# Group norm statistics with tokens on partitions, a first norm that multiplies by its weights in rows, and a new order of the mixer's pieces

## The chip, the cores and the metric

The kernel runs on one core of a Trainium2 chip. The metric is device time in microseconds (us) of one execution. TensorE (PE, with PEld for its weight loads), VectorE (DVE), ScalarE (ACT), GpSimd (POOL) and SyncE (SP, which here only issues DMAs) each work through a queue of their own; data moves between HBM and on-chip memory by DMA.

## The reference

One encoder layer on x of 512 tokens by 1024 channels, all float32. Cut to what matters here:

```python
def rmsnorm(x, w):
    y = x * rsqrt(mean(x * x, axis=-1) + 1e-5)
    return y * w

h = rmsnorm(x, norm1_w)
p = h @ w_in                      # 1024 -> 2464: r, k, v, decay, a, gate, pool
# token shift of the RWKV columns, RWKV-7 scan in two directions (8 heads of 64),
# multi-scale pooling of the last 512 columns
y = wkv(...)                      # (tokens, 8 heads, 64)
y = (y - y.mean(-1)) / sqrt(y.var(-1) + 64e-5) * ln_x_w + ln_x_b   # per token and head
y = (y + bonus) * g               # g: a gate from two small products
x = x + concat(y, pooled) @ w_out
# then RMSNorm, a PEER layer (16384 single-neuron experts, top 16 of 8 heads),
# residual, final RMSNorm
```

## The kernel before

The mixer (up to about 435 us of the span) holds activations with channels on partitions and the 512 tokens along the free axis, in four token tiles x0 to x3 of 128. Matrices that must be exact are split into a high part and the rest, and a product is the sum of three passes: `wh*hh`, `wh*hl`, `wl*hh`.

**Norm 1 (lines 224 to 245).** Per token tile: ACT squares the 128x1024 tile and sums it (L234), `rstd_of` makes 1/rms out of it (L153 on DVE, L155 a square root on ACT, L157 on DVE), DVE multiplies the tile by it (L236), PE turns it over in eight 128x128 transposes, DVE multiplies by norm1_w out of PSUM into `hf` (L242), ACT rounds `hf` to `hh` (L244) and DVE or POOL, by a string, makes `hl = hf - hh` (L245). This block has no order of its own: the framework's scheduler places it. The last tile's L236 comes behind much of the other tiles' work.

**The mixer's streams.** After norm 1 the mixer is a set of generators, each of which issues one piece of work per step. A string PROG names, letter by letter, which generator takes its next step, and within it PE, DVE, ACT, SP and POOL keep exactly that order. The letters that matter here:

- `m`: the 20 column tiles of the input projection ("products", L338 to L342, in the order PORD; weight fetch L325, split L332 on ACT and L335 on DVE or POOL by the string WL). `0` to `3`: elementwise work of one of four head pairs (ct), in two directions (string EW says which of its operations go to POOL). `p`: pooling.
- `s`/`S`: the triangular solves of head pairs 0 and 1 / 2 and 3. They load AU from DRAM (L599) and do 31 pairs of small DVE steps (L607, L609). `j`/`J`: what is joined to them on PE.
- `h`: four gates (L857, L858, copied by ACT in L859). `l`: w_out (wo) and the residual (xr) by DMA on POOL's queue. `f`, `o`, `X`, `Y`: the output projection (L843) by parts.
- `a`, `b`: the two chains of eight chunks (L731 to L795; each chunk needs GA and UV from DRAM), of heads 0 to 3 and 4 to 7. `n`, `x`, `y`: group norm of heads 0 to 3 for all 512 tokens (`n`), of heads 4 to 7 for the middle 256 tokens (`x`) and for the outer 256 (`y`).

**Group norm (L806 to L835).** Mean by a matmul with `bm`, subtracted (L815); squares on ACT (L820); the sums over each head's 64 channels by a matmul with `hsel` as stationary operand (L821), which leaves heads on partitions: 8 x 512 or 8 x 256. On it DVE adds eps (L824), ACT takes the root (L825), DVE the reciprocal (L826). A matmul with `hselT` (L830) spreads it over the channels, times ln_x_w; L832 to L834 apply it, with ln_x_b, bonus and gate.

The PEER part behind the mixer is about 1275 us of the span and isn't touched.

Of the kernel before, what the change touches and what calls it, by code (L numbers as in the profile page):

```python
# [10 lines left out]
F32 = mybir.dt.float32  # L11
# [4 lines left out]
AF = mybir.ActivationFunctionType  # L16
# [42 lines left out]
WL = 'VVVGVGGGGVGVVVGVGVGG'  # L59
EW = 'VVGVVVVVVGVVGVGVVGVGVVVGVGGVVVGVGVGVGGGGVVVGGGVGGGVG'  # L60
# [100 lines left out]
def mixer(ctx, rs, tc, t, x_dram, x2_dram, ident, vec, vecs, dbg, load_vectors):  # L161
# [56 lines left out]

    with ExitStack() as s1:
        ld = s1.enter_context(tc.tile_pool(name="ld", bufs=1, side="right"))  # L220
        st = s1.enter_context(tc.tile_pool(name="st", bufs=NST, side="right"))
        x = [ld.tile([128, D], F32, name=f"x{i}") for i in range(NT)]
        XQ = {"S": (SY, SY), "A": (SY, A)}[QX]

        one = st.tile([128, 1], F32, name="one", bufs=1)
        V.memset(one, 1.0)
        A.activation(one, one, AF.Sqrt)
        for i in range(NT):
            XQ[i % 2].dma_start(x[i], x_dram[:, i])
        load_vectors()  # L230
        for i in range(NT):
            sc = st.tile([128, D], F32, name="sc", bufs=2)
            ssq = st.tile([128, 1], F32, name="ssq")
            A.activation(sc, x[i], AF.Square, accum_out=ssq)  # L234
            r = rstd_of(nc, st, ssq, "n1", 1.0 / D, RMS_EPS, 1)
            (G if SX[i] == "G" else V).tensor_scalar(x[i], x[i], r, None, op0=ALU.mult)  # L236
            for q in range(2):
                pt = bank([128, 4, 128])
                for d in range(4):
                    PE.transpose(pt[:, d], x[i][:, (4 * q + d) * 128:(4 * q + d + 1) * 128], ident)  # L240
                hf = st.tile([128, 4, 128], F32, name="hf", bufs=NHF)
                V.tensor_tensor(hf, pt, vecs("n1")[:, 4 * q:4 * q + 4, None].to_broadcast([128, 4, 128]), op=ALU.mult)  # L242
                part = lambda z: z[:, 4 * q:4 * q + 4, i * 128:(i + 1) * 128]
# [13 lines left out]
    rkh = mc.tile([128, 4], F32, name="rkh")
    V.tensor_scalar(rkh, vecs("rk"), 0.5, None, op0=ALU.mult)
    mln2 = mc.tile([128, 1], F32, name="mln2")
    V.memset(mln2, -float(np.log(2.0)))  # L260

    cmask = mc.tile([128, NC, C], F32, name="cmask")
    V.memset(cmask, 1.0)
    V.memset(cmask[:, :, 0:1], 0.0)
    cmaskf = cmask.rearrange("p c t -> p (c t)")

    gm = mc.tile([128, 2, C], F32, name="gm")
    V.memset(gm, 1.0)
    for hf in range(2):
        for k in range(2):  # L270
            G.affine_select(gm[hf * 64:hf * 64 + 64, k, :], gm[hf * 64:hf * 64 + 64, k, :], [[1, C]], ALU.is_ge, 0.0,
                            base=-1 if k == 0 else 0, channel_multiplier=-1)
    gmask = gm.rearrange("p k t -> p (k t)")


    hsel = mc.tile([128, 4, H], F32, name="hsel")
    sel2 = mc.tile([128, 2], F32, name="sel2")
    seli = mc.tile([128, 4, 8], F32, name="seli")
    bones = mc.tile([128, 128], F32, name="bones")
    for z in (hsel, sel2, seli, bones):  # L280
        G.memset(z, 0.0)
    for hf in range(2):
        rows = slice(hf * 64, hf * 64 + 64)
        V.memset(sel2[rows, hf:hf + 1], 1.0)
        V.memset(bones[rows, hf * 64:hf * 64 + 64], 1.0)
# [1323 lines left out]
```

## Time and profile before

| | |
|---|---|
| runs | 1709.47, 1710.9, 1721.64 us; median 1710.9 |
| profiled execution | 1711.15 us, span 1709.4 us, mean granted clock 0.962 |
| busy over the span | PE 1586.8 us (93%), DVE 1288.1 (75%), ACT 668.9 (39%), POOL 520.4 (30%) |
| first projection's first matmul | 21.90 us |
| solve 0 | steps from 187.56 us |
| chain 0, chain 1 | from about 291 us, from about 356 us |
| last output projection ends | about 435 us |

A row of the timeline gives the start, the duration, the engine, the line and the operation with its output and input; brackets give the engine's idle time before it and what ended that. Where matmuls stand one behind another a row's time is that of the whole run. The granted clock (PEclk) is a share of TensorE's 2.4 GHz; the two levels are 1.2 and 2.4 GHz, and a value between is a stretch with both.

### The profile page before, as it was taken

The numbers are of one execution on the slowest core, as the hardware profiler recorded it, in microseconds if no ns is written. First come the engines' busy times: TensorE is split into PE (matmuls) and PEld (weight loads), VectorE is DVE, ScalarE is ACT, GpSimd is POOL, SyncE is SP. The second block draws the span as 40 slices with busy tenths as digits, with TensorE's granted clock in tenths as the row PEclk, the third lists the DMA queues.
The fourth block names the chain that finished last, engine by engine and source line by source line (L and its number), as shares of the span: only waits on it lengthen the run. The fifth ranks groups of instructions, "written<-read, shape, count | busy, mean of one in ns | idle before, by whom it ended". The sixth has DMA issues, their size and how long they took to land.

```text
span 1709.4 us, 26365 instructions
## 1 busy us (share of the span) xinstructions
PE 1586.8 (93%) x9809; PEld 1326.2 (78%) x9809; DVE 1288.1 (75%) x2595; ACT 668.9 (39%) x1115; POOL 520.4 (30%) x359
## 2 busy tenths in 40 slices
PE   6898557989999699999999999999999999999997
PEld 5676444564787478988898989999998989999886
DVE  5557777346689999996567777877778877887776
ACT  4455322121333377774333333333333333333334
POOL 2313242000122000011024544445445555454430
PEclk8899778998999899999999999999999999999999
DMA  3344469671321365567979988989988998886774
GB/s 133 110 144 117 131 168 313 166 240 54 116 84 58 107 246 212 207 234 273 327 246 330 341 302 331 338 296 333 345 309 322 345 327 304 318 327 239 274 259 154
DMA packets 220193, 405.32 MB, mean 237 GB/s; under 512 B 38352, under 2 KB 137168, under 8 KB 216992
## 3 DMA queue, kind: packets, MB, share of 16 engines
q1 hardware_dynamic: 179536, 257.53, 45.7%
q0 software_dynamic: 39952, 145.05, 23.2%
q8 instruction: 77, 1.26, 0.3%
q10 hardware_dynamic: 576, 1.05, 0.2%
q14 instruction: 52, 0.43, 0.1%
HBM read 350.23 MB, written 53.35 MB: 236 GB/s over the span
## 4 chain that ended last, share of the span: by engine, by line
PE 63%; DVE 19%; DMA 5%; issue 1%; ACT 1%; SPq 1%; POOL 0%; DVEq 0%; ACTq 0%
PE o L1456 30%; PE d L1029 7%; PE d L1028 7%; PE d L1027 7%; PE mm L843 3%; DMA gt<-gdram 2%; DVE ul L1015 2%; DVE a L1256 1%; DMA UV<-vd 1%; DVE b L1258 1%; DVE bh L1260 1%; DVE pr L1530 1%; DVE tmf L607 1%; DVE i L1489 1%; DVE i L1486 1%
## 5 line engine op out<-in xcount | busy, mean ns | idle before, releaser
L1027 PE MATMUL d<-hh,uh 128*128 128x384 f32 x968 | 329.3, 340 | 0.3 <-ACT uh L1013 0.3
L1029 PE MATMUL d<-hh,ul 128*128 128x384 f32 x968 | 328.2, 339 | 1.1 <-DVE ul L1015 1.1
L1028 PE MATMUL d<-hl,uh 128*128 128x384 f32 x968 | 327.0, 338 | 0.0
L1373 POOL DMA_INDIRECT gat<-in_peer_u,num x128 | 192.3, 1502 | 291.7 <-DVE gat L1379 238.6
L1373 POOL DMA_INDIRECT gat<-in_peer_v,num x128 | 199.2, 1556 | 212.8 <-DVE acc L1381 193.2
L1456 PE MATMUL o<-vh,wh 128*128 128x512 f32 x768 | 238.4, 392 | 2.3 <-ACT wh L1440 2.3
L1456 PE MATMUL o<-vl,wh 128*128 128x512 f32 x768 | 238.5, 392 | 1.6 <-DVE vl L1015 1.5
L1456 PE MATMUL o<-vh,wl 128*128 128x512 f32 x768 | 238.6, 392 | 0.0
L1013 ACT CAST uh<-ur 128x1024 fp32r<-128x1024 f32 x121 | 127.2, 1051 | 258.9 <-PE d L1028 254.1
L1440 ACT CAST wh<-gl 128x384 fp32r<-128x384 f32 x128 | 65.7, 514 | 308.4 <-PE o L1456 297.3
L1028 PEld LDWEIGHTS d<-hl,uh 128*128 128x128 f32 x968 | 182.1, 188 | 4.2
L1027 PEld LDWEIGHTS d<-hh,uh 128*128 128x128 f32 x968 | 182.1, 188 | 3.9 <-ACT uh L1013 0.5
L1029 PEld LDWEIGHTS d<-hh,ul 128*128 128x128 f32 x968 | 182.1, 188 | 2.1 <-DVE ul L1015 1.8
L1442 DVE TENSOR_TENSOR wl<-gl,wh 128x384 fp32r<-128x384 f32 x128 | 71.3, 558 | 139.5 <-ACT wh L1440 139.4
L1015 DVE TENSOR_TENSOR ul<-ur,uh 128x1024 fp32r<-128x1024 f32 x121 | 147.7, 1221 | 37.1 <-ACT uh L1013 36.5
L1456 PEld LDWEIGHTS o<-vl,wh 128*128 128x128 f32 x768 | 144.1, 188 | 34.5 <-DVE vl L1015 3.1
L1456 PEld LDWEIGHTS o<-vh,wl 128*128 128x128 f32 x768 | 144.5, 188 | 31.2
L1381 DVE SCALAR_TENSOR_TENSOR acc<-gat,wg,acc 128x1024 f32<-128x1024 f32 x128 | 163.9, 1280 | 0.9
L1456 PEld LDWEIGHTS o<-vh,wh 128*128 128x128 f32 x768 | 143.6, 188 | 26.6 <-ACT wh L1440 2.6
L1015 DVE TENSOR_TENSOR vl<-vr,vh 128x1024 fp32r<-128x1024 f32 x128 | 156.2, 1221 | 8.5 <-ACT vh L1013 8.1
L1379 DVE SCALAR_TENSOR_TENSOR gat<-gat,h2g 128x1024 f32<-128x1024 f32 x128 | 153.6, 1219 | 0.0
L1013 ACT CAST vh<-vr 128x1024 fp32r<-128x1024 f32 x128 | 135.1, 1055 | 23.2 <-DMA vr<-in_peer_v 21.3
(374 smaller groups left out, 2457.8 us busy)
## 6 DMA issues: line engine op xcount, KB each, us to landing
ur<-in_uT SPq DMA_DIRECT2D x128, 512.0 KB, 5.0
vr<-in_peer_v SPq DMA_DIRECT2D x128, 512.0 KB, 3.6
gdram<-sg SPq DMA_DIRECT2D x24, 1024.0 KB, 5.6
gt<-gdram SPq DMA_DIRECT2D x16, 1536.0 KB, 11.3
wqk<-in_wqk SPq DMA_DIRECT2D x16, 576.0 KB, 3.8
gad<-gs SPq DMA_DIRECT2D x16, 512.0 KB, 3.5
GA<-gad SPq DMA_DIRECT2D x16, 512.0 KB, 5.7
w<-in_w_in SPq DMA_DIRECT2D x15, 512.0 KB, 4.8
```

The costliest lines, as they stand in the source:

```text
L843: PE.matmul(ps, (ocm if d < 4 else ypool)[:, d % 4, i * 128:(i + 1) * 128], wo[:, d, h], start=d == ds[0], stop=d == ds[-1])
L1013: A.copy(hi, src)
L1015: eng.tensor_tensor(lo, src, hi, op=ALU.subtract)
L1027: PE.matmul(ps, uh[:, c], hh[:, d, 0:ND], start=d == 0, stop=False)
L1028: PE.matmul(ps, uh[:, c], hl[:, d, 0:ND], start=False, stop=False)
L1029: PE.matmul(ps, ul[:, c], hh[:, d, 0:ND], start=False, stop=d == DT - 1)
L1373: G.indirect_dma_start(out=u, out_offset=None, in_=t["peer_u" if k < NP else "peer_v"], in_offset=bass.IndirectOffsetOnAxis(ap=num[:, kk:k ...
L1379: V.scalar_tensor_tensor(u, u, 1.0, h2g, op0=ALU.mult, op1=ALU.mult, accum_out=dot[:, kk:kk + 1])
L1381: V.scalar_tensor_tensor(acc, u, wg[:, kk:kk + 1], acc, op0=ALU.mult, op1=ALU.add)
L1440: A.copy(wh, w)
L1442: wi = V.tensor_tensor(wl, w, wh, op=ALU.subtract)
L1456: PE.matmul(O[j][q], a[:, c], b[:, q * 512:(q + 1) * 512], start=e == 0 and n == 0, stop=e == NE - 1 and n == 2)
```

## The change

What it does:

1. **Norm 1.** norm1_w is loaded as a row repeated over 128 partitions (`n1`, 512 KB, the second DMA on SP, ahead of x1). One DVE instruction per tile multiplies by 1/rms and by `n1`. `hf` is gone: ACT copies `hh` straight out of PSUM, DVE makes `hl` out of PSUM and `hh`; none goes to POOL. The block gets an order: all four `normed`, then tiles 0 and 1 turned over, the first weight split, tiles 2 and 3. The first weight fetches come ahead of the small constants.
2. **The first product** is done in two halves of 256 columns (48 matmuls of 128x256 for 24 of 128x512), and by passes, so that the first half needs tiles 0 and 1 alone.
3. **Group norm.** The squares are the stationary operand and `sel2` (128x2) the moving one: tokens on partitions, 128x8 for 256 tokens of four heads. Then eps, root, reciprocal on 128x8, a transpose to 8x128, an ACT copy, and four matmuls with `gselT`. A piece is always 256 tokens, so `n` has two pieces.
4. **A new PROG**, with other WL, EW, PORD and BP. Group norm's pieces stand further ahead among the chunks of chain 1.

```diff
-WL = 'VVVGVGGGGVGVVVGVGVGG'
+WL = 'VVVGVVGGGGGVVVGVGVGG'
-PORD = [12, 13, 4, 0, 8, 15, 5, 1, 2, 6, 16, ...
+PORD = [12, 13, 4, 0, 8, 15, 5, 1, 6, 2, 16, ...
-BP = 'GAGAVAVV'
+BP = 'GAGGVAVG'
-PROG = '...mwmmvpggvDjpjjSSSSSSSSSChhSSSSSlaSSSSlffffff...
+PROG = '...mwmpmvgvDpjjChhhjSSSSSSSSSSSSSSSSSSSlShhalffffff...
...
-            r = rstd_of(nc, st, ssq, "n1", 1.0 / D, RMS_EPS, 1)
-            (G if SX[i] == "G" else V).tensor_scalar(x[i], x[i], r, None, op0=ALU.mult)
-            for q in range(2):
...
-                hf = st.tile([128, 4, 128], F32, name="hf", bufs=NHF)
-                V.tensor_tensor(hf, pt, vecs("n1")[:, 4 * q:4 * q + 4, None].to_broadcast([128, 4, 128]), op=ALU.mult)
-                A.copy(part(hh), hf)
-                (G if SH[2 * i + q] == "G" else V).tensor_tensor(part(hl), hf, part(hh), op=ALU.subtract)
+        n1 = st.tile([128, D], F32, name="n1w", bufs=1)
+        SY.dma_start(x[0], x_dram[:, 0])
+        SY.dma_start(n1, bass.AP(tensor=t["norm1_w"].tensor, offset=t["norm1_w"].offset, ap=[[0, 128], [1, D]]))
+        for i in range(1, NT):
+            SY.dma_start(x[i], x_dram[:, i])
+        fetch(PORD[0])
+        load_vectors()
+        fetch(PORD[1])
+        with in_order(tc, V.engine, A.engine, PE.engine):
+            def normed(i):
...
+                V.scalar_tensor_tensor(x[i], x[i], r, n1, op0=ALU.mult, op1=ALU.mult)
+            def turned_over(i):
+                for q in range(2):
...
+                    A.copy(part(hh), pt)
+                    V.tensor_tensor(part(hl), pt, part(hh), op=ALU.subtract)
+            turned(selT, seli)
+            for i in range(NT):
+                normed(i)
+            for i in range(NT):
+                if i == 2:
+                    ready[PORD[0]] = weights(PORD[0])
+                turned_over(i)
...
+    def early_product(wh, wl, ps):
+        for n in range(2):
+            c = slice(n * 256, n * 256 + 256)
+            for k, (w, h) in enumerate(((wh, hh), (wl, hh), (wh, hl))):
+                for d in range(DT):
+                    PE.matmul(ps[:, c], w[:, d], h[:, d, c], start=k == d == 0, stop=k == 2 and d == DT - 1)
...
-            sq = wo_p.tile([128, 512], F32, name="sq2", bufs=2)
+            sq = wo_p.tile([128, 256], F32, name="sq2", bufs=2)
             A.activation(wide(sq), part(ocm[:, ct]), AF.Square)
-            PE.matmul(pv_[0:H, :n], hsel[:, ct, :], sq[:, :n], start=ct == cts[0], stop=ct == cts[1])
+            for k in range(2):
+                PE.matmul(pv_[:, k, ct % 2], sq[:, k * 128:(k + 1) * 128], sel2, start=True, stop=True)
-        nr = wo_p.tile([H, 512], F32, name="nr2")[:, :n]
-        V.tensor_scalar(nr, pv_[0:H, :n], 1.0 / N, GN_EPS, op0=ALU.mult, op1=ALU.add)
+        nr = wo_p.tile([128, 8], F32, name="nr2")
+        V.tensor_scalar(nr, pv_.rearrange("p i c h -> p (i c h)"), 1.0 / N, GN_EPS, op0=ALU.mult, op1=ALU.add)
         A.activation(nr, nr, AF.Sqrt)
         V.reciprocal(nr, nr)
         yield
+        pn = bank([128, 512], ps_mm)[0:8, 0:128]
+        PE.transpose(pn, nr, ident)
+        nt = wo_p.tile([8, 128], F32, name="nt2")
+        A.copy(nt, pn)
+        yield
         for ct in cts:
-            PE.matmul(pb[:, :n], hselT[:, ct, :], nr, start=True, stop=True)
+            for k in range(2):
+                PE.matmul(pb[:, k * 128:(k + 1) * 128], gselT[g][:, 2 * k + ct % 2], nt, start=True, stop=True)
...
-        ("n", gnorm(0, slice(0, 4)), "ah"),
+        ("n", linked([gnorm(0, slice(1, 3)), gnorm(0, slice(0, 4, 3))]), "ah"),
```

How the order moves at three places. The first is SP's queue in front of solve 0: `ard` is a write that waits for an elementwise result, AU what solve 0 begins with. Before:

```order
L325 DMA w<-in_w_in 128x1024
L531 DMA btd<-bt 128x8x128
L481 DMA ard<-ar 128x8x128
L599 DMA AU<-da 32x1024 x4
L556 DMA da<-gs 32x8x32 x2
```

Now:

```order
L224 DMA w<-in_w_in 128x1024
L554 DMA btd<-bt 128x8x128
L622 DMA AU<-da 32x1024 x4
L504 DMA ard<-ar 128x8x128
L579 DMA da<-gs 32x8x32 x2
```

AU has moved ahead of one `ard`. On DVE one head group's pooling (13 instructions, five of them on about 512 columns) and two `ar` of 128x512, which POOL did, now stand ahead of solve 0's first step.

The second is PE ahead of chain 0, whose first matmuls are those `c<-UV,GA`. L857 and L858 are a gate, L843 (L873 now) the output projection. Before:

```order
L652 MATMUL a<-W_1887,ZT 32x32 x32
L857 MATMUL mm<-gd,cp 128x512
L858 MATMUL mm<-gd_90,cp 128x512
L843 MATMUL mm<-wo,ypool 128x512 x6
L731 MATMUL c<-UV,GA 64x64 x8
L843 MATMUL mm<-wo,ypool 128x512
L764 MATMUL c<-RV_2294,W_1887 64x64 x8
L731 MATMUL c<-UV,GA 64x64 x8
```

Now:

```order
L675 MATMUL a<-W_1869,ZT 32x32 x64
L887 MATMUL mm<-gd,cp 128x512
L888 MATMUL mm<-gd_90,cp 128x512
L887 MATMUL mm<-gd,cp 128x512
L888 MATMUL mm<-gd_90,cp 128x512
L887 MATMUL mm<-gd,cp 128x512
L888 MATMUL mm<-gd_90,cp 128x512
L887 MATMUL mm<-gd,cp 128x512
L888 MATMUL mm<-gd_90,cp 128x512
L873 MATMUL mm<-wo,ypool 128x512 x6
L754 MATMUL c<-UV,GA 64x64 x8
```

Three of the four gates stood inside chain 0; now all four come ahead of it.

The third is DVE in the last chunks of chain 1, around group norm of heads 0 to 3. L778 to L795 (L803 and on now) are the chain's own, L824, L826 and L832 to L834 group norm's. Before:

```order
L771 TENSOR_TENSOR X_3475<-X_3393,lc 128x256
L824 TENSOR_SCALAR nr_3477<-mm 8x512
L826 RECIPROCAL nr_3477<-nr_3477 8x512
L780 TENSOR_TENSOR X_3475<-X_3475,c 128x256
L794 TENSOR_TENSOR ocm<-ocm,o 128x2x64
L795 TENSOR_TENSOR ocm<-ocm,o 128x2x64
L832 TENSOR_TENSOR ocm<-ocm,mm 128x512
```

Now:

```order
L794 TENSOR_TENSOR X_3417<-X_3333,lc 128x256
L862 TENSOR_TENSOR ocm<-ocm,mm 128x256
L863 SCALAR_TENSOR_TENSOR ocm<-ocm,pv,bon 128x256
L864 TENSOR_TENSOR ocm<-ocm,gate 128x256
L862 TENSOR_TENSOR ocm<-ocm,mm 128x256
L863 SCALAR_TENSOR_TENSOR ocm<-ocm,pv,bon 128x256
L864 TENSOR_TENSOR ocm<-ocm,gate 128x256
L837 TENSOR_TENSOR ocm<-ocm,mm 128x2x128
L803 TENSOR_TENSOR X_3417<-X_3417,c 128x256
```

The reciprocal that stood ahead of a step of the chain is now one chunk earlier and on 128x8; in this chunk seven operations of group norm stand ahead of the chain's L803.

## Rows read from the trace of the kernel before

**Rows 1.** Timeline of 0 to 36 us, all engines; columns as told above.

```profile
4.37 1.06 ACT L234 ACTIVATE sc<-x 128x1024 f32<-128x1024 f32 x1 [2.06 <-DMA x<-in_x]
...
8.78 1.04 ACT L234 ACTIVATE sc<-x 128x1024 f32<-128x1024 f32 x1
...
16.90 1.81 DVE L236 TENSOR_SCALAR x<-x,n1o 128x1024 f32<-128x1024 f32 x1
...
21.90 0.80 PE L340 MATMUL mm<-hh,wh 128*128 128x512 f32 x1 [0.25 <-ACT hh L244]
...
24.06 0.63 PE L340 MATMUL mm<-hh,wh 128*128 128x512 f32 x1
...
24.48 0.63 PE L341 MATMUL mm<-hl,wh 128*128 128x512 f32 x1
...
29.36 0.39 PE L340 MATMUL mm<-hh,wh 128*128 128x512 f32 x1
...
29.59 0.39 PE L341 MATMUL mm<-hl,wh 128*128 128x512 f32 x1
...
30.92 0.69 ACT L348 ACTIVATE wd<-mm,c 128x512 f32<-128x512 f32 x1 [8.47 <-PE mm L342]
```

**Rows 2.** One line's instructions by shape: count, ns min/median/max, first and last start.

```profile
L1110 DVE SCALAR_TENSOR_TENSOR xr<-xr,n2o,n x3: 1276/1279/1285, 427.2 to 437.2; 128x1024 f32<-128x1024 f32 x3
...
L1118 ACT CAST hh<-mm x8: 586/587/591, 435.4 to 448.0; 128x512 fp32r<-128x512 f32 x8
...
L1119 DVE TENSOR_TENSOR hl<-mm,hh x8: 681/684/692, 436.0 to 448.7; 128x512 fp32r<-128x512 f32 x8
...
L430 DVE RECIPROCAL nr<-nr x4: 202/203/203, 48.5 to 175.3; 128x8 f32<-128x8 f32 x4
...
L826 DVE RECIPROCAL nr<-nr x3: 1741/1741/3341, 382.4 to 420.3; 8x256 f32<-8x256 f32 x2, 8x512 f32<-8x512 f32 x1
...
L426 PE MATMUL a<-sel,sq x32: 165/251/272, 46.6 to 170.2; 128*128 128x2 f32 x32
...
L484 DVE SCALAR_TENSOR_TENSOR b<-at,kap x8: 668/684/1771, 60.3 to 229.9; 128x512 f32<-128x512 f32 x8
...
L522 POOL TENSOR_TENSOR bp<-bk,lc x2: 1907/1916/1924, 75.1 to 143.9; 128x1024 f32<-128x1024 f32 x2
```

**Rows 3.** Stretches: length; busy time and instructions of each engine; granted clock; DMA.

```profile
60.00:170.00 110.00, 96.33 (x513) 72.62 (x511) 65.95 (x105) 53.48 (x94) 34.57 (x21) 0.94 0.48 135
...
190.00:240.00 50.00, 25.28 (x129) 18.24 (x130) 46.72 (x92) 11.39 (x25) 13.83 (x9) 0.74 0.46 119
...
292.00:355.00 63.00, 60.54 (x1012) 36.10 (x1010) 27.84 (x69) 10.72 (x29) 0.00 (x0) 0.93 0.66 194
...
380.00:400.00 20.00, 15.39 (x84) 7.20 (x84) 12.27 (x18) 2.71 (x5) 0.00 (x0) 0.66 0.11 34
```

**Rows 4.** Timeline of 174 to 188 us, SP's queue and DVE.

```profile
176.07 0.74 SPq L481 DMA_DIRECT2D ard<-ar  x1
...
176.86 4.64 SPq L599 DMA_DIRECT2D AU<-da  x4
...
180.64 0.75 DVE L452 SCALAR_TENSOR_TENSOR kap<-k,pv,a 128x512 f32<-128x512 f32 x1 [2.23 <-PE a L450]
...
187.56 0.19 DVE L607 TENSOR_TENSOR tmf<-WU,AU 128x31 f32<-128x31 f32 x1 [2.38 <-DMA AU<-da]
```

**Rows 5.** Timeline of 272 to 292 us, PE.

```profile
272.15 2.07 PE L857 MATMUL mm<-gd,cp 128*128 128x512 f32 x2
...
274.02 1.91 PE L858 MATMUL mm<-gd,cp 128*128 128x512 f32 x2
...
290.64 0.44 PE L731 MATMUL c<-UV,GA 64*64 64x64 f32 x2 [5.35 <-DMA UV<-vd]
```

**Rows 6.** Timeline of 376 to 436 us, DVE and PE.

```profile
385.76 2.07 PE L830 MATMUL mm<-nr,hselT 8*128 8x512 f32 x2 [4.05 <-DVE nr L826]
...
424.38 10.57 PE L843 MATMUL mm<-wo,ocm 128*128 128x512 f32 x24
```

More of the change, by code (lines that the diff above doesn't have):

```diff
@@ L257, in mixer @@
[L257 to L285, printed above, removed]
-        for i in range(4):
-            V.memset(hsel[rows, i, 2 * i + hf:2 * i + hf + 1], 1.0)
-            V.memset(seli[rows, i, 2 * i + hf:2 * i + hf + 1], 1.0)
@@ L289, in mixer @@
-    bm = mc.tile([128, 128], F32, name="bm")
-    V.tensor_scalar(bm, bones, 1.0 / N, None, op0=ALU.mult)
-    selT = mc.tile([8, 4, 128], F32, name="selT")
-    hselw = mc.tile([128, 4, H], F32, name="hselw")
-    for ct in range(4):
-        V.tensor_scalar(hselw[:, ct], hsel[:, ct], vec("lnw", ct), None, op0=ALU.mult)
-    def turned(dst, src):
-        pt = bank([128, 4, 128])
-        for ct in range(4):
-            PE.transpose(pt[0:8, ct], src[:, ct, :], ident)
-        V.tensor_copy(dst, pt[0:8])
@@ L336, in weights @@
         return wh, wl
+    mln2 = mc.tile([128, 1], F32, name="mln2")
+    V.memset(mln2, -float(np.log(2.0)))
+    cmask = mc.tile([128, NC, C], F32, name="cmask")
+    V.memset(cmask, 1.0)
+    V.memset(cmask[:, :, 0:1], 0.0)
+    cmaskf = cmask.rearrange("p c t -> p (c t)")
+    gm = mc.tile([128, 2, C], F32, name="gm")
+    V.memset(gm, 1.0)
+    for hf in range(2):
+        for k in range(2):
+            G.affine_select(gm[hf * 64:hf * 64 + 64, k, :], gm[hf * 64:hf * 64 + 64, k, :], [[1, C]], ALU.is_ge, 0.0,
+                            base=-1 if k == 0 else 0, channel_multiplier=-1)
@@ new lines, in mixer @@
+    gmask = gm.rearrange("p k t -> p (k t)")
+    sel2 = mc.tile([128, 2], F32, name="sel2")
+    seli = mc.tile([128, 4, 8], F32, name="seli")
+    bones = mc.tile([128, 128], F32, name="bones")
+    for z in (sel2, seli, bones):
+        G.memset(z, 0.0)
+    for hf in range(2):
+        rows = slice(hf * 64, hf * 64 + 64)
+        V.memset(sel2[rows, hf:hf + 1], 1.0)
+        V.memset(bones[rows, hf * 64:hf * 64 + 64], 1.0)
+        for i in range(4):
+            V.memset(seli[rows, i, 2 * i + hf:2 * i + hf + 1], 1.0)
@@ new lines, in mixer @@
+    lw = keep.tile([128, 2, 512], F32, name="lw")
+    SY.dma_start(lw[:, 0], t["w_up"])
+    SY.dma_start(lw[:, 1], t["a_up"])
+    pw = mc.tile([128, 4, 128], F32, name="pw")
+    edge = mc.tile([128, 4, 16], F32, name="edge")
+    GAd = dram.tile([NC, 128, 16, 2 * C], F32, name="gad")
+    ARd = dram.tile([NC, 128, 2, 4, 2 * C], F32, name="ard")
+    BTd = dram.tile([NC, 128, 2, 4, 128], F32, name="btd")
+    Vd = dram.tile([2, S, 512], F32, name="vd")
+    DA = dram.tile([2, 2, 8, NC, 32, 32], F32, name="da")
@@ L382, in products @@
             ps = bank([128, 512], ps_mm)
-            for k, _ in enumerate(product(*ready.pop(ct), ps)):
+            for k, _ in enumerate((product if n else early_product)(*ready.pop(ct), ps)):
                 if k == 1 and n + 1 < len(order):
@@ L912, in swap_late @@
         wo = wo_p.tile([128, DT, D], F32, name="wo")
-        hselT = wo_p.tile([H, 4, 128], F32, name="hselT")
-        turned(hselT, hselw)
+        gselT = [wo_p.tile([8, 4, 128], F32, name=f"gselT{g}") for g in range(2)]
+        for g in range(2):
+            turned(gselT[g], seliw[:, g])
         bonus(2)
```

114 lines of the change are left out of this document (57 added, 57 removed).

## The prediction

> **What bounds the kernel now.** I read the busy times of the stretches first, because the share over the whole span hides that the mixer's stages have different limits. From 60 to 170 us PE is busy for 96 of 110 us and DVE for 66: the projection sets the pace, DVE is its second limit. From 190 to 240 us it is the other way round, DVE 46.7 of 50 us, PE 25.3: the small steps of solve 0 and the elementwise work beside them. From 292 to 355 us PE is busy 60.5 of 63 us: chain 0. From 380 to 400 us PE has 15.4 of 20 us, at a granted clock of 0.66 [rows 3]. Then I read the timeline at the seams, where the idle time of an engine and its releaser say what is late: the front, the wait for AU, the wait for UV, group norm. Everything behind the mixer waits for its output, so a time saved there should reach the end whole.
>
> **The front.** Before, the first product starts at 21.90 us and its result is used at 30.92 [rows 1]. It starts so late because the fourth tile is scaled only at 16.90 us, though ACT squares the tiles from 4.37 us on and the last, I take from the rhythm, is the one at 8.78. Now the four tiles go first. One DVE operation of 1.28 us (its like: L1110 [rows 2]) takes the place of the scaling and of two multiplications out of PSUM. Tile x1 comes one transfer later, since `n1` goes ahead of it; I give it 1 us. A tile then takes DVE 1.9 us with its three small steps, and the four are scaled by about 13.8 us. ACT copies hh of tiles 0 and 1, four times 0.59 us [rows 2], but behind the last root (the last square at 9.8, 1.04 long, so about 11.5), thus to 13.9, and splits the weight (1024 columns, at that rate 1.1 us) by some 15.5. The first half of the product starts there, not at 21.90. DVE has four hl of 0.68 us and wl, at that rate 1.3, behind 13.8 us, done near 17.8, which the second pass just waits for. A 512-column matmul steps 0.42 us at the start (24.06 to 24.48) and 0.23 late (29.36 to 29.59) [rows 1]. So 24 matmuls of 256 columns take 5.1 us at the low clock, to about 21 us with a wait, and the other 24 take 2.8 us at the high one: 23.8 us. That is 7 us before 30.92. Bounds: all at the low clock and a start at 17 us end at 27.5 (gain 3.4); hl and wl without a wait end near 22 (gain 9). I take **-7**. DVE gains cover too: POOL no longer makes hl.
>
> **The middle, 30 to 170 us.** The products' order and the elementwise pieces change places. POOL gets two more `bp` of 1.9 us (L522) and one more small operation; DVE loses as much. A DVE operation of 0.68 us lasts up to 1.77 us where POOL works beside it (L484: minimum, median and maximum [rows 2]), so moving work to POOL isn't free: 1.1 us for each operation that is hit. The Trainium skill, "GPSIMD Engine Reference", section 1 (Specifications), says that POOL's SBUF interfaces are shared with VectorE and contend with DVE instructions that read two SBUF inputs. The trace agrees; if by that rule each microsecond of POOL blocked DVE, the three operations would cost 5 us and the sum below would be 3 less. By the row I book 2 hits, **+2**, from -2 (DVE's relief counts) to +6 (five hits).
>
> **Solve 0.** DVE waits 2.23 us ahead of L452 and 2.38 ahead of L607, between 180 and 188 us, while AU is on the way; AU is issued at 176.86 us behind an `ard` at 176.07 [rows 4]. Moving AU ahead of it saves that queue step, 0.8 us, no more, because the writes that AU reads stand ahead of both. The rest of the wait is now filled: one head group's pooling, five operations of about 0.68 us each (as L1119 [rows 2], 512 columns) and small ones, about 4 us, and two `ar`, 1.4 us, stand ahead of the first step. Work that fills a wait leaves the solve's own stretch, which is bound by DVE [rows 3]. But it stands ahead of the scan whose results the roots wait for, so part of it only shifts the wait. I take **-4**; bounds 0 (all shifted) and -6 (pooling, ar and the queue step whole, less the transfer itself).
>
> **Gates.** A gate is four matmul passes, two each for L857 and L858. They take 2.07 + 1.91 us at the low clock [rows 5] and, at the late rate of 24 passes in 10.57 us [rows 6], 1.76 at the high one. Three of four move out of chain 0, which is bound by PE [rows 3], into the wait for UV, of which 5.35 us are idle in one piece [rows 5]. Out of chain 0 goes 3 x 1.76 = 5.3 us. Into the wait come 5.3 us if the clock has risen, up to 12 if not; in the second case some 6 us stick out. Busy matmuls should also carry the high clock into chain 0, which starts low now. I take **-5**, from -7 to 0.
>
> **Group norm and the tail.** The reciprocals cost 3.34 us once and 1.74 twice (L826 [rows 2]); on 128x8 one costs 0.20 (L430), so 6.8 us become 0.8 for four pieces. DVE isn't the bound here as a whole; what counts is PE's wait of 4.05 us for the first reciprocal and the low clock after it: 380 to 400 us at 0.66, thus about two thirds of it at half speed [rows 3, 6], and that is some 5 us lost on 11 us of matmuls. On PE the sums cost about the same (matmuls with two moving columns last 0.25 us and overlap, L426 [rows 2]; four of them take the place of two with 256), the spreading loses its 512-column pieces at the low clock, about 2 us. Together up to -12. Against it: each piece has two hops more (transpose, ACT copy), and on DVE seven operations of group norm, about 3 us, now stand ahead of the chain's L803 in one chunk, with PE waiting for that. +3 to +4. I take **-8**, from -13 to -2.
>
> **Sum.** -7 + 2 - 4 - 5 - 8 = -22. From the profiled execution's 1711.15 us, which is the median of 1710.9 but for 0.25 us, it makes 1689 us.
>
> **Rivals.**
> - *The front's gain is caught by a later wait.* The middle has a second limit in DVE, and the solve's inputs come through POOL and SP. If pooling ahead of the scan and POOL's extra work shift AU's chain by as much as the front gives, then -7 and -4 go and -13 stays, less 2 for the hits: about 1698 to 1700. For it: DVE sits at 66 of 110 us with waits [rows 3]. Against: PE is the busier there. Chance 0.25.
> - *The tail turns cold.* Place: PE from 380 us on. Four pieces have each a chain PE, DVE, ACT, DVE, PE, ACT, PE of some 2.5 us (a reciprocal of 0.2 us, a root and a copy hardly longer, two matmul hops, and the handoffs: an estimate). Should nothing cover it, PE idles 10 us, and the granted clock stays at 1.2 GHz as it did around the 4.05 us wait. The tail's matmuls, some 40 us of the 55 from 380 to 435, then take up to 20 us more: +30 in the place of -8, thus 1689 + 38 = 1727 at the worst, and slower than before from 22 us on, that is when about half of the tail runs at the low clock and the waits aren't covered. The Trainium skill, "TensorE: Matmul & The Clock Gate", section "HAM oscillation — how this bites in real kernels", has this as a rule: waits between bursts of matmuls throttle the clock again each time. The trace shows it once in the tail [rows 3, 6]. Against: the new order puts chain steps and projections between the hops. Chance 0.07, with about 1716.
> - *Group norm's change doesn't reach the end.* If the last projection waits for chain 1 itself, whose chunks need their transfers, the shorter norm only adds idle time: -22 + 8 = 1697. For it: chain 1 is a sequence of dependent steps. Against: at 355 to 435 us PE is busy nearly throughout, so its work and clock count. Chance 0.10.
>
> The forecast has the rest, 0.58, with 1689 and an own range of 1676 to 1699.
>
> **Chances and range.** 1% is 17 us, about what a measurement of this kernel surely tells from no change; faster means under 1694, slower over 1728. Faster: 0.54 of the forecast's 0.58, a third of the first rival (0.08), a third of the third (0.03): 0.65. Slower: the worst end of the second rival and what I haven't seen, 0.05. Same: 0.30. The bounds added up linearly give -37 to +1, but they hardly all fall together; with the first and third rival inside, the range is 1674 to 1705.
>
> **What would show it.** Front: the first result read near 24 us, the product starting near 15.5; wrong if it starts after 18. Middle: the last gs of head pair 1 some 5 to 7 us earlier than before; if it is at the same time, the first rival holds. Solve 0: DVE without waits of 2 us ahead of its first step, and fewer us from there to the solve's end. Gates: four in a row ahead of chain 0, and its stretch shorter by 5 us; wrong if chain 0's first UV lands before the gates are done. Tail: no reciprocal over 0.3 us, no PE wait of 4 us, a granted clock near 1 from chain 1 to the end of the projection, which comes 8 us sooner after chain 1's start than before; wrong if the clock falls there or PE's waits on DVE's L803 add up to more than 5 us. PEER: the same length within 2 us; if not, something is off that I don't see.

## The result, and the profile after

The changed kernel takes 1693.26 us (median of 8 runs, 1690.51 to 1702.58); the kernel before, in as many runs beside it, 1710.64. The ratio is 0.9893, with a 95% interval of 0.9872 to 0.9914: 1.1% faster, 17.4 us by the medians. Measured a second time it took 1691.48 against 1711.67 us (ratio 0.9882). The forecast was 1689 us, -22, with a range of 1674 to 1705. The profiled span is 1693.8 us, 15.6 less than before, and the stages are compared by it. The events are starts; the solve's end is the start of the copy AU<-WU behind its last step.

| event | before | now | now - before | by itself | forecast |
|---|---|---|---|---|---|
| first product's reader (ACT wd) | 30.92 | 23.25 | -7.7 | -7.7 | -7 |
| solve 0's first step | 187.56 | 176.82 | -10.7 | -3.1 | +2, with a part of -4 |
| solve 0's end | 239.80 | 226.51 | -13.3 | -2.6 | the rest of -4 |
| first gate | 272.15 | 260.24 | -11.9 | +1.4 | 0 |
| chain 1, its first p<-X,AR | 358.63 | 340.82 | -17.8 | -5.9 | -5 |
| first transpose behind the mixer | 434.79 | 417.87 | -16.9 | +0.9 | -8 |
| end of the span | 1709.4 | 1693.8 | -15.6 | +1.3 | 0 |

The first view is the timeline of the front, which answers to [rows 1]; the product's matmuls of one pass and half are one row of eight.

```profile
4.36 1.06 ACT L298 ACTIVATE sc<-x 128x1024 f32<-128x1024 f32 x1 [1.82 <-DMA x<-in_x]
...
7.85 1.06 ACT L298 ACTIVATE sc<-x 128x1024 f32<-128x1024 f32 x1 [1.92 <-DMA x<-in_x]
...
13.29 1.28 DVE L300 SCALAR_TENSOR_TENSOR x<-x,n1o,n1w 128x1024 f32<-128x1024 f32 x1
...
16.43 1.19 PE L359 MATMUL mm<-hh,wh 128*128 128x256 f32 x8
...
18.15 1.21 PE L359 MATMUL mm<-hh,wl 128*128 128x256 f32 x8 [0.53 <-DVE wl L234]
...
23.25 0.69 ACT L373 ACTIVATE wd<-mm,c 128x512 f32<-128x512 f32 x1 [4.42 <-PE mm L359]
```

The row added ahead of x1 delays its squares by 2 us (7.85 us against 5.85), not by 1. The fourth tile is nevertheless scaled at 13.29 us, not at 16.90. The first half begins at 16.43, and its second pass waits half a microsecond for wl. Eight matmuls of 256 columns take 1.0 us from row to row (19.20 to 20.16 and 20.16 to 21.12, not shown), and the granted clock from 14 to 28 us is 1.00: the high clock from the start, where I had the low one for the first half.

At solve 0 (answering to [rows 4]) SP's queue and DVE, in the timeline. First the last transfer that AU waits for, in the kernel before:

```profile
171.30 1.82 SPq L556 DMA_DIRECT2D da<-gs  x2
```

and now that transfer, AU and what stands on DVE ahead of the first step:

```profile
156.18 1.78 SPq L579 DMA_DIRECT2D da<-gs  x2
...
158.99 0.71 DVE L688 TENSOR_TENSOR pb<-pa 128x527 f32<-128x527 f32 x1 [4.10 <-ACT pa L390]
...
160.87 3.22 SPq L622 DMA_DIRECT2D AU<-da  x4
...
174.75 0.75 DVE L475 SCALAR_TENSOR_TENSOR kap<-k,pv,a 128x512 f32<-128x512 f32 x1 [2.23 <-PE a L473]
...
176.82 0.19 DVE L630 TENSOR_TENSOR tmf<-WU,AU 128x31 f32<-128x31 f32 x1
```

AU is now issued 16 us ahead of the first step, and the wait of 2.38 us for it is gone; the wait of 2.23 us in the chain of roots stays, and a new one of 4.10 us stands ahead of the pooling, whose input ACT copies out of a product. The transfer `da<-gs` is issued 15.1 us earlier than before, the first step starts only 10.7 us earlier. Ahead of chain 0 (answering to [rows 5]), PE in the timeline:

```profile
260.24 1.12 PE L887 MATMUL mm<-gd,cp 128*128 128x512 f32 x2
...
266.35 1.02 PE L888 MATMUL mm<-gd,cp 128*128 128x512 f32 x2
267.21 5.31 PE L873 MATMUL mm<-wo,ypool 128*128 128x512 f32 x12
272.45 0.68 PE L754 MATMUL c<-UV,GA 64*64 64x64 f32 x16
...
281.62 0.70 PE L801 MATMUL c<-UV,BT 128*64 128x64 f32 x8 [5.08 <-DVE UV L789]
```

All four gates run at the high clock, 0.86 us for each pair of passes. The wait that follows is 5.08 us, but it isn't the one of [rows 5] for UV's transfer: it is for a DVE operation (L789), which stands in DVE's queue behind steps of the solve, in the same timeline:

```profile
280.71 0.39 DVE L632 TENSOR_TENSOR WU<-WU,tmf 128x220 f32<-128x220 f32 x1
281.13 0.43 DVE L789 TENSOR_SCALAR UV<-c 64x256 f32<-64x256 f32 x1
```

The tail, in stretches (columns as in [rows 3]), first of the kernel before, from chain 1's first p<-X,AR on:

```profile
358.60:380.00 21.40, 19.99 (x456) 14.62 (x456) 9.01 (x21) 6.23 (x19) 0.00 (x0) 1.00 0.90 278
...
400.00:435.00 35.00, 34.08 (x203) 15.68 (x203) 26.38 (x52) 9.17 (x19) 0.80 (x2) 1.00 0.26 97
```

Between these two lies the stretch of [rows 3] with 15.39 of 20 us at 0.66. The changed kernel:

```profile
340.80:358.00 17.20, 13.53 (x333) 11.25 (x333) 6.58 (x17) 6.08 (x18) 0.00 (x0) 1.00 0.89 273
358.00:378.00 20.00, 18.29 (x197) 13.65 (x197) 10.36 (x29) 3.42 (x10) 0.00 (x0) 0.66 0.34 107
378.00:418.00 40.00, 39.09 (x262) 19.82 (x262) 24.75 (x53) 8.86 (x20) 0.80 (x2) 1.00 0.22 84
```

PE's idle time in the tail was 1.4 + 4.6 + 0.9 = 6.9 us and is 3.7 + 1.7 + 0.9 = 6.3; its busy time was 69.5 us and is 70.9, with some fifty matmuls more; twenty microseconds at 0.66 are there in both. What PE waits for there, now (in all, times, longest; it answers to the 4.05 us of [rows 6]):

```profile
PE mm L845 <- ACT sq L843: 2.0, 3, 0.8
PE c L754 <- DMA UV<-vd: 1.5, 2, 1.0
PE c L801 <- DVE UV L789: 0.6, 1, 0.6
...
PE mm L853 <- DVE nr L850: 0.3, 1, 0.3
```

The one long wait has become many short ones, for squares and for chain 1's transfers, none over 1.0 us, and the clock fell all the same, behind a stretch in which PE was busy for 13.5 of 17.2 us.

### The profile page after: what moved, and what is told of

Read it like the earlier page. It is cut to its first block, busy times and chain, and to the rows that moved or that the text cites. A ratio compares the mean times of both kernels' runs of the same rounds, so it can differ in the third digit from the quotient of the medians.

```text
span 1693.8 us, 26505 instructions
## 1 busy us (share of the span) xinstructions
PE 1579.8 (93%) x9885; PEld 1333.0 (79%) x9885; DVE 1283.2 (76%) x2596; ACT 664.8 (39%) x1114; POOL 518.3 (31%) x357
## 3 DMA queue, kind: packets, MB, share of 16 engines
q0 software_dynamic: 39952, 145.05, 23.3%
## 4 chain that ended last, share of the span: by engine, by line
PE 62%; DVE 17%; DMA 5%; issue 1%; ACT 1%; SPq 1%; POOL 0%; DVEq 0%; ACTq 0%; POOLq 0%
PE o L1485 28%; PE d L1058 8%; PE d L1056 8%; PE d L1057 8%; PE mm L873 3%; DMA gt<-gdram 2%; DVE ul L1044 1%; DMA vr<-in_peer_v 1%; DVE a L1285 1%; DVE b L1287 1%; DVE bh L1289 1%; DVE pr L1559 1%; DVE tmf L630 1%; DVE i L1518 1%; DVE s L1516 1%
## 5 line engine op out<-in xcount | busy, mean ns | idle before, releaser
L1485 PEld LDWEIGHTS o<-vh,wl 128*128 128x128 f32 x768 | 144.5, 188 | 31.1
L1408 DVE SCALAR_TENSOR_TENSOR gat<-gat,h2g 128x1024 f32<-128x1024 f32 x128 | 153.6, 1220 | 0.0
```

The lines of the kernel that those rows point to most:

```text
L1408: V.scalar_tensor_tensor(u, u, 1.0, h2g, op0=ALU.mult, op1=ALU.mult, accum_out=dot[:, kk:kk + 1])
L1485: PE.matmul(O[j][q], a[:, c], b[:, q * 512:(q + 1) * 512], start=e == 0 and n == 0, stop=e == NE - 1 and n == 2)
```

## The experiments

Each is told with its median and, where it was timed, its ratio to the kernel before on the same chip (the changed kernel's first was 0.9893). The stretches of their profiles stand in one table: "front" is the first product's reader, the others are the lengths from it to solve 0's first step, from solve 0's end to the first gate, from there to chain 1, and from there to the end of the last output projection.

| kernel | front | to solve 0 | to gate | to chain 1 | tail |
|---|---|---|---|---|---|
| before | 30.9 | 156.6 | 32.4 | 86.5 | 76.3 |
| changed; again | 23.3; 23.1 | 153.6; 155.1 | 33.7; 31.2 | 80.6; 79.2 | 77.2; 78.3 |
| new front alone; again | 23.4; 23.3 | 156.4; 155.1 | 40.5; 40.3 | 85.1; 85.7 | 76.3; 77.2 |
| new group norm alone | 29.4 | 156.2 | 33.9 | 87.3 | 79.7 |
| changed, old front | 30.7 | 155.7 | 29.6 | 85.6 | 77.7 |
| changed, first product whole | 28.1 | 156.7 | 29.7 | 89.3 | 74.8 |
| changed, old group norm | 23.2 | 154.0 | 30.5 | 80.6 | 83.9 |
| changed, gates late | 23.3 | 154.4 | 32.7 | 86.8 | 76.8 |
| changed, old tables | 23.3 | 157.7 | 31.1 | 79.9 | 81.2 |
| changed, 6; 9; 12 moved | 23.3 (all) | 152.8; 154.0; 154.1 | 30.9; 31.3; 30.8 | 75.7; 76.9; 73.1 | 79.0; 78.1; 79.2 |

Kernels with the same instructions in a stretch differ there by 2 to 4 us, on the way to chain 1 by up to 10 and in the tail by up to 6: a smaller difference between two profiles proves nothing by itself. The tail of the new group norm alone holds, unlike the others, the first transposes behind the mixer (told there).

**The new front alone.** Against the kernel before:

```diff
-    with ExitStack() as s1:            # norm 1, channels' weights out of PSUM
+    with ExitStack() as s1:            # normed() x4, turned_over(), weights, turned_over()
-            for k, _ in enumerate(product(*ready.pop(ct), ps)):
+            for k, _ in enumerate((product if n else early_product)(*ready.pop(ct), ps)):
```

> The kernel before with norm 1 by rows and the halved first product, and nothing else of the change (order strings, tables and group norm as before). In the changed kernel the first product's reader starts 7.7 us sooner. Theory: nothing behind it catches this up, because PE and DVE work in that stage and no transfer sets a time: the whole gets 6.5 to 8 us faster, about 1703. Rival: a later wait (AU ahead of solve 0, UV ahead of chain 0) takes it back: 0 to -3 us, 1708 or more, and the first solve step starts no more than 3 us sooner.

1709.99 us, ratio 0.9977 (0.9956 to 0.9997): the rival's size, and not by its mechanism. The gain is whole at solve 0's first step (-7.8) and at its end; behind it 8 us go, between the solve's end and the first gate. There PE is idle 5.7 us longer than in the kernel before, at a granted clock of 0.84 against 0.92. The timeline of PE shows most of it: seven matmuls of a run wait 3.94 us with no releaser, and the product behind them steps 0.43 us at first, the low clock. A second profile of the same kernel was to tell chance from place.

> The kernel before with the new front alone, a second look. The first lost 6.5 of its 7.7 us behind solve 0 at a PE wait of 3.9 us, with no releaser in the trace and an instruction fetch inside it. Theory: the fetch meets the transfers of that moment, and how long it takes is chance: the wait is under 2 us this time, and the stretch from solve 0's end to chain 0's first matmul near 43 us, the time 1703 to 1705. Rival: that place makes PE wait each time: a wait of 3 to 4 us there again, the time 1708 or more.

1710.43 us, one execution. PE's timeline in this second profile:

```profile
246.61 2.35 PE L666 MATMUL a<-ZT,A 32*32 32x32 f32 x121
252.90 0.42 PE L666 MATMUL a<-ZT,A 32*32 32x32 f32 x7 [3.94 <-issue]
253.25 0.80 PE L365 MATMUL mm<-hh,wh 128*128 128x512 f32 x1
```

and in the first one:

```profile
254.37 0.42 PE L666 MATMUL a<-ZT,A 32*32 32x32 f32 x7 [3.94 <-issue]
```

The same seven matmuls, the same 3.94 us: that speaks for the place and against chance, by two profiles. In both, one packet of an instruction queue falls into the wait. The DMA view of the first profile, cut to 250.4 to 254.4 us (queue, packets, MB, share of 16 engines):

```profile
q1 hardware_dynamic: 3386, 0.43, 104.0%
q0 software_dynamic: 77, 0.18, 13.8%
q8 instruction: 1, 0.02, 1.8%
```

That PE waits for its own instructions behind a full set of DMA engines fits this. So does the end of these waits: between solve 0's end and chain 1, ten PE waits of more than 1.1 us have no releaser, in seven of the fourteen profiles, and each ends 1.3 to 1.7 us after such a packet does (1.60 and 1.62 us for the two of 3.94). It was not tried, and it stays an inference. No other kernel here has such a wait of more than 1.8 us.

**The changed kernel with the old front.**

```diff
-        with in_order(tc, V.engine, A.engine, PE.engine):   # new norm 1, early_product
+        for i in range(NT):                                 # norm 1 and product as before
```

> The changed kernel with the norm 1 and the undivided first product of the kernel before: new order, tables and group norm stay. Put alone into the kernel before, the new front had its 7.7 us until solve 0 ended and lost 6.5 of them behind it, at a wait of 3.9 us on PE for which the trace names no cause and the low clock after it. Theory: that loss is that kernel's own; here the front is worth what it gains at its place, so this one is 6.5 to 8.5 us slower than the changed kernel, about 1700. Rival: a later wait behind solve 0 absorbs what comes earlier, in any order: within 3 us of the changed kernel.

1702.17 us, ratio 0.9942 (0.9918 to 0.9967), 8.9 us over the changed kernel. The reader is 7.5 us late, solve 0's first step 9.6, and the difference at the end is of that size. So in the new order the front's gain reaches the end. (Its chain 0 is 5 us longer and its way to the gate 4 us shorter, with no instruction changed; I don't read these.)

**The first product in one piece.**

```diff
-            for k, _ in enumerate((product if n else early_product)(*ready.pop(ct), ps)):
+            for k, _ in enumerate(product(*ready.pop(ct), ps)):
```

> The changed kernel with its first product in one piece of 512 columns (three passes for each 128 rows of weights in turn), so that it waits for all four tiles. Theory: it can begin when the last hl is there, at 20.5 us, and takes 5.5 us at the high clock: its reader starts at 26 to 26.5, 3 us later than in the changed kernel, and the whole is 2 to 3.5 us slower, about 1696. Rival 1: PE idles from 17 to 20 us, the clock falls and the product takes 9 us: its reader starts near 29, 5 to 6 us slower. Rival 2: what comes later here is taken up behind: within 1 us.

1701.45 us, ratio 0.9944 (0.9926 to 0.9962); its reader starts at 28.07, 4.8 us late: the first rival, at the front. PE's timeline:

```profile
17.41 0.49 PE L365 MATMUL mm<-hh,wh 128*128 128x512 f32 x1 [0.97 <-ACT hh L308]
19.90 0.79 PE L366 MATMUL mm<-hl,wh 128*128 128x512 f32 x1 [2.00 <-DVE hl L309]
20.49 0.63 PE L367 MATMUL mm<-hh,wl 128*128 128x512 f32 x1
20.92 0.63 PE L365 MATMUL mm<-hh,wh 128*128 128x512 f32 x1
```

After the waits of 0.97 and 2.00 us the matmuls step 0.43 us, the low clock, up to 25 us. The halves keep PE at work there and the clock high: 4.8 of the front's 7.7 us hang on them. About half of that is the clock: twelve matmuls at 0.43 us in the place of 0.23 make 2.4 us, an estimate from these steps; the rest is the later start.

The whole is 8.2 us slower, more than that rival's 5 to 6. In this profile the way from the first gate to chain 1 is 8.7 us longer than in the changed kernel, with one long wait of PE:

```profile
289.23 1.41 PE L754 MATMUL c<-UV,GA 64*64 64x64 f32 x16 [9.43 <-DMA UV<-vd]
```

No instruction is changed there, and why this transfer comes late I can't say. So the whole doesn't measure the halves alone; the reader does.

**The old form of group norm in the new order,** one piece of 512 tokens for heads 0 to 3:

```diff
-        ("n", linked([gnorm(0, slice(1, 3)), gnorm(0, slice(0, 4, 3))]), "ah"),
+        ("n", gnorm(0, slice(0, 4)), "ah"),
-            PE.matmul(pv_[:, k, ct % 2], sq[:, k * 128:(k + 1) * 128], sel2, ...)
+            PE.matmul(pv_[0:H, :n], hsel[:, ct, :], sq[:, :n], ...)
```

> The changed kernel with the old form of group norm: heads 0 to 3 in one piece of 512 tokens with heads on partitions, the steps at the places of the new order. The new form alone in the old order made the tail 3.5 us longer. Theory A: the form is worth nothing by itself, PE's waits and the low clock only change place: within 2 us of the changed kernel. Theory B: in the new places, where its hops lie between chain steps, the new form is worth the PE wait of 4 us and the low clock behind it: 4 to 8 us slower than the changed kernel, with a PE wait of 3 to 4 us for a reciprocal.

1698.74 us, ratio 0.9922 (0.9893 to 0.9952), 5.5 us over the changed kernel, and its tail is 83.9 us long. PE's waits in it (in all, times, longest):

```profile
PE mm L853 <- DVE nr L849: 5.6, 2, 3.9
PE mm L844 <- ACT sq L843: 1.3, 2, 1.1
```

Theory B: in the new places the form is worth 5.5 us in all (7.3 against the changed kernel's second median). The tail is longer than each of the six with the new form in the same places (74.8 to 81.2 us), PE is idle in it for 12.4 us against 6.3 and 5.6 in the changed kernel's two profiles, and the wait for the reciprocal is the one of the kernel before. The old form comes with its piece of 512 tokens; form and size of the pieces are not told apart.

**The new form alone in the old order.**

```diff
-        ("n", gnorm(0, slice(0, 4)), "ah"),
+        ("n", linked([gnorm(0, slice(1, 3)), gnorm(0, slice(0, 4, 3))]), "ah"),
-...aaaabbbbbbbbbbbnbbbbnbnbnbnbnbnnxooooo...
+...aaaabbbbbbbbbbbnnbbbbnnbnnbnnbnnbnnbnnnnnnxooooo...
```

> The kernel before with group norm's new form alone (tokens on partitions, pieces of 256), its steps at the places that the old order gives them. In the changed kernel the stretch from chain 1's start to the first transposes behind the mixer took 77.0 us, 76.2 before. Theory A: the form is worth little wherever it stands, since PE waits for more hops and its clock falls all the same: -2 to +2 us. Theory B: the form is worth the forecast 6 to 9 us, and the new places of its pieces among chain 1's chunks gave that back: -6 to -9 us here, with no granted clock below 0.9 behind chain 1.

1712.96 us, ratio 1.0012 (0.9991 to 1.0032), 1.9 us over the kernel before and not separated from no change: theory A. With two steps at each old place the hops stand back to back, and PE waits for them: it is idle for 7.2 us of the tail (6.9 before), the longest wait now 1.1 us, at the same granted clock of 0.91. The tail of 79.7 us, 3.4 longer than before, is no measure here: the first transposes behind the mixer stand ahead of its last projections (429.6 and 438.8 us). From chain 1's start to the end of the span it is 1350.8 us in both.

**The gates back inside chain 0.**

```diff
-...DpjjChhhjSSSSSSSSSSSSSSSSSSSlShhalffffffhaSfSSafSaSSfSSSf...
+...DpjjChhjSSSSSSSSSSSSSSSSSSSlSalffffffaShfSSahfShaShSfSSSf...
```

> The changed kernel with three of the four gates back inside chain 0, where the old order had them. Theory: chain 0 is bound by PE, so the gates' 5.3 us come back: 5 to 6 us slower than the changed kernel, about 1699, and from the first gate to chain 1's start as long as before. Rival: the 5.9 us that this stretch got shorter come from elsewhere (the wait for UV, the clock): within 1.5 us of the changed kernel.

1698.95 us, ratio 0.9911 (0.9877 to 0.9944); from the first gate to chain 1 86.8 us, as before the change, against 80.6 and 79.2. The theory, by the size of the whole. PE in that stretch, the changed kernel and this one (columns as in [rows 3]):

```profile
260.24:340.82 80.58, 71.93 (x1141) 42.38 (x1137) 46.00 (x116) 13.64 (x37) 5.38 (x8) 0.94 0.77 232
```

```profile
260.05:346.80 86.75, 71.99 (x1140) 41.86 (x1136) 46.28 (x117) 13.64 (x37) 5.39 (x8) 0.92 0.70 215
```

PE is busy for as long and idle for 14.8 us in the place of 8.6: the gates ahead of chain 0 fill a wait, as the theory has it. The length of the stretch by itself would not do: two other kernels with early gates have 85.6 and 89.3 us there, at a lower granted clock (0.90 and 0.92 against 0.94 and 0.98).

**The old tables.**

```diff
-WL = 'VVVGVVGGGGGVVVGVGVGG'
+WL = 'VVVGVGGGGVGVVVGVGVGG'
-BP = 'GAGGVAVG'
+BP = 'GAGAVAVV'
# and EW of before
```

> The changed kernel with the tables of the kernel before that say which elementwise and splitting operations go to POOL (WL, EW, BP); the order of the pieces stays new. From the first product's reader to solve 0's first step the changed kernel takes 153.6 us, the kernel before 156.6. Theory A: moving the work to POOL at the right places made those 3 us: here 156 to 157 us, and 2 to 4 us slower than the changed kernel in all. Theory B: the order made them (fewer products ahead of solve 0), and POOL's extra operations stretch DVE's: within 1.5 us of the changed kernel, or up to 3 us faster.

1696.04 us, ratio 0.9905 (0.9872 to 0.9938); to solve 0 157.7 us, against 152.8 to 155.1 in the seven profiles with the new tables and the whole new front (155.7 and 156.7 with parts of the old one). That speaks for theory A, though not far outside the scatter. A cut at the last `da<-gs` ahead of AU says it more clearly. Here that row is

```profile
164.11 1.78 SPq L579 DMA_DIRECT2D da<-gs  x2
```

140.9 us behind the first product's reader. With the old tables, in either order, it is 138.8 to 140.9 us (five profiles), with the new ones 132.2 to 136.0 (nine): the tables are worth 5 to 9 us up to there. From there to solve 0's end the kernels of the old order take 68.5 to 68.7 us, those of the new order 70.3 with the new tables and 66.5 with the old ones. So the order is worth 2.0 us there, and the tables cost 3.8: two `ar` stand on DVE, and the pooling waits 4.10 us for its product, here 1.83. The whole is 2.8 to 4.6 us over the changed kernel's two medians; its tail, with the low clock for 24 us, adds to that by chance or not.

**Pooled projection matmuls moved from chain 0 into chain 1,** six, twelve and nine of 32 (letters f of the order, set between those of n):

```diff
-...afafflaffaaafJfaffafaaalabbbbbbbbbnbnbnbbnnbnbnnnnbnnnbnbnnbnn...
+...afafflafaaaJaaaaalabbbbbbbbbnbnfbnbbnfnbnfbnnfnnfbnnfnbnbnnbnn...
```

> The changed kernel with the last six matmuls of the output projection's pooled half (5.3 us of PE) taken out of chain 0 and put between group norm's steps in chain 1. Theory: in chain 1 PE waits for some 5 us of 28 and then works 13.7 us at the low clock; the six matmuls fill the waits: chain 0 gets 5 us shorter, the tail 0 to 2 us longer, 3 to 5 us faster than the changed kernel in all, about 1689, and the low clock behind chain 1 shorter. Rival: PE's waits there are the chain's own steps in sequence and every inserted matmul delays one: what chain 0 gains the tail loses, within 1.5 us of the changed kernel.

> As the kernel with six pooled projection matmuls moved from chain 0 into chain 1, now twelve (10.6 us of PE). Theory: the first six filled most of the waits (the low clock behind chain 1 fell from 13.7 us to 6.8), so twelve bring 0 to 2 us more than six, about 1688. Rival: the tail has room for all of them: another 3 to 4 us, about 1685, and no low clock behind chain 1.

> The changed kernel with nine of the pooled projection's matmuls in chain 1 in the place of chain 0 (six gave 1688.6 us, twelve 1689.5). Theory: PE's idle time behind chain 1's start, 7.5 us, and the low clock are what is to be had, and six to twelve are on its flat part: 4 to 6 us faster than the changed kernel on the same chip, 1688 to 1689. Rival: the two earlier results were the chip's: within 2 us of the changed kernel.

> The changed kernel once more, to stand on the same chip beside the next one. The median so far is 1693.3 us; another 1692 to 1696, with the low clock behind chain 1 again for 10 to 14 us.

Medians 1688.64 (ratio 0.9863, 0.9820 to 0.9906), 1689.49 (0.9881, 0.9850 to 0.9913) and 1690.63 us; the changed kernel beside the last 1691.48, both with ratio 0.9882. By the profiles the first theory holds: the way to chain 1 gets 2 to 8 us shorter, the tail 0 to 2 longer, and the granted clock of the whole tail rises. The stretch from chain 1 to the end, changed kernel and again:

```profile
340.80:418.00 77.20, 70.90 (x790) 44.72 (x791) 41.69 (x98) 18.35 (x48) 0.80 (x2) 0.91 0.40 132
```

```profile
338.30:416.60 78.30, 72.73 (x790) 47.30 (x791) 41.64 (x98) 18.15 (x48) 0.80 (x2) 0.87 0.39 130
```

and with six, then twelve moved:

```profile
332.40:411.40 79.00, 71.10 (x800) 44.36 (x801) 43.01 (x100) 18.20 (x48) 0.80 (x2) 0.96 0.40 130
```

```profile
330.90:410.10 79.20, 73.83 (x814) 43.74 (x813) 43.85 (x101) 18.12 (x48) 0.80 (x2) 1.00 0.37 122
```

0.91 and 0.87 become 0.96 and 1.00 (0.98 with nine), while the tail holds 5 to 11 us of matmuls more. What is left of the low clock with six stands at chain 1's very start; behind it is

```profile
344.50:411.40 66.90, 61.75 (x608) 36.09 (x607) 39.34 (x92) 15.85 (x40) 0.80 (x2) 1.00 0.33 112
```

In all six profiles of that tail with none moved the granted clock falls to 0.57 or less over some 4 us behind the first 12 us of chain 1; in the three with matmuls moved it doesn't. But PE's idle time in the tail, 6.3 and 5.6 us, is 7.9 with six and 5.4 with twelve: that the moved matmuls fill waits in sum, as the theory has it, isn't shown.

By the clock on the wall less is certain: beside the changed kernel nine moved gained 0.9 us, within the scatter, where I expected 4 to 6. That is the size of the rival. The profiles of that pair differ by 2.7 us. Twelve gave no more than six, though the low clock was gone. The changed kernel's second run missed both of my marks by a little: 1691.48 us, not 1692 or more, and, by the mean of 0.87, some 20 us at the low clock in its tail, not 10 to 14. The three are the lowest medians here; that they beat the changed kernel isn't separated from noise.

## Why the prediction was right, and where it wasn't

**Front, -7: right** (-7.7), with two errors that cancel in part, which is luck: the product started at 16.43, not 15.5, and ran at the high clock throughout. The first rival's loss is real in another kernel (the front alone), at a place and by a wait that I had not named; in the new order it doesn't occur.

**Middle, +2: wrong in sign.** Up to the last `da<-gs` ahead of AU, where the prediction put the sign of this term, the way from the first product's reader is 7.5 us shorter, and that row comes 15.1 us earlier, where I had 5 to 7. I booked POOL's added operations as hits on DVE. They are there: bp on POOL takes 1.93 us, four times. But the old tables in the new order bring the 7.5 us back, so the new split gains there. Counting operations that move to POOL doesn't tell whether they stood on the path.

**Solve 0, -4: wrong, +1.8**, from that row to the solve's end (68.5 us before, 70.3 now), though the table of events hides it. Some parts came as booked: moving AU ahead of the `ard` saved 0.9 us between that row and AU's issue (4.7 us, 5.6 before), the wait for AU is gone, and the solve's own steps are 2.6 us shorter. What failed is that the filling work costs nothing: the pooling itself waits 4.10 us for its product, and with the two `ar` the way from that row to the first step takes 20.6 us, 16.3 before. The new tables make this; with the old ones the new order has 66.5, half of the term.

**Gates, -5: right** in size, -5.9, and undoing it costs 5.7 us in all. In the new order the gates fill a wait: back inside chain 0 they leave PE idle for 6 us more. Against the kernel before only 1.5 us of the 5.9 are idle time (10.1 and 8.6 us); the rest is PE's work, 76.4 us then and 71.9 now, at a granted clock of 0.94 in the place of 0.89. The prediction had named the clock, without a price. Kernels with these gates lie at 79.2 to 89.3 us in this stretch, so a hit within 1 us is luck too.

**Tail, -8: the step that failed.** It measured +0.9 (+2.0 in the second profile of the kernel). The prediction said that the wait of 4.05 us and the low clock behind it go, and that the spreading gets 2 us cheaper. The wait went; other waits of together 3.5 us took its place, as many as the part against it had booked. The low clock, priced at 5 us, stayed: twenty microseconds at 0.66, as before. And PE's busy time didn't fall, it rose by 1.5 us, with some fifty matmuls more. What the form and its places are worth the two experiments show: in the new places the form is worth 5.5 us (5.6 to 6.7 of tail: 83.9 us with the old form there), in the old ones nothing that can be read. The new places with the old form are 7.6 us of tail longer than the kernel before, by one profile each. The term added the form's worth to the old tail and took too little off for moving its steps into chain 1. That this is so because PE's steps there are short and wait on each other is my reading and not shown. The third rival, group norm not reaching the end, had 1697 by that; the second, a cold tail, has half its mechanism here, though the clock was no lower than before. By the Trainium skill's "TensorE: Matmul & The Clock Gate", section "HAM oscillation — how this bites in real kernels", waits between bursts throttle the clock again. The trace of the kernel before agrees, with a wait of 4.05 us and 0.66 in that stretch; the changed kernel has the same 0.66 with no wait over 1.0 us in its tail.

PEER, from the end of the mixer on, is 1.3 us longer in this profile; over all kernels with the new group norm in the new order it lies between 1274.1 and 1276.0 us, before it was 1274.5: scatter.

So the sum came out near by luck: the middle and solve 0 together gave 3.7 us more than booked (-5.7 for -2), the front and the gates some 1 us each, and that paid for 5.3 of the 8.9 us missing in the tail. The way to the first gate, +1.4, and PEER, +1.3, are within scatter.

## What to carry to other kernels

Before a chain of small steps is made shorter, ask what the engine that waits for it does meanwhile: here the shorter chain was worth 5 us or nothing, by where its steps stood in the order. Try independent work of the waiting engine in its waits, and judge by that engine's idle time and granted clock over the whole stage, not by the one longest wait. Where a stage begins cold, split the first piece of work so that it can start on half its inputs: that was worth 4.8 us at its place, about half of it by the clock. And work moved into a wait must itself have its inputs there: the pooling ahead of solve 0 waited 4.10 us for its own.

## What the runs showed that I had not expected

- A wait of PE of 3.94 us without releaser, at the same seven matmuls in two profiles of one kernel and in none of the other twelve, with an instruction packet inside it and all DMA engines busy. If it is the fetch, moving instructions can cost by where they put such a place; 8 us in that stretch here, other waits and the low clock behind it included.
- With the first product whole, behind PE waits of 0.97 and 2.00 us at 17 to 20 us, the granted clock fell to 0.50 (20 to 24 us); with the halves' matmuls there it stayed at 1.00. PE had done little but transposes before in both.
- In a stretch with the same instructions the low clock lasts differently from kernel to kernel: the tail's granted clock was 0.91 (twice), 0.87, 0.89, 0.95 and 0.83 with the same tail order, and its length 74.8 to 81.2 us.
